# Attention units of a hybrid trunk issued from the memory's K/V projections on, with a second clock for ScalarE

## The chip, the cores and the metric

The kernel runs on one core of one Trainium2 chip (trn2). The metric is the device time of one execution in microseconds. Three executions of the kernel before gave 1529.0, 1531.52 and 1532.66; a profile of one execution stands behind all rows below.

## The reference

One decoder layer on 1024 tokens of 1024 features, all in float32. What the change touches is the first sub-layer and a part of the second:

```
a = rmsnorm(x, g_mix);  proj = a @ w_in          # q, k, v | u, v of the gating | gates
# 12 heads of 64 in 3 groups, (window, dilation) = (128,1), (512,4), (2048,16)
s = q.k * 64**-0.5 + alibi bias, masked to the window
e = exp(s - max);  den = sum(e);  o = (e @ v) / den;  lse = max + log(den)
y_attn = sum over groups of softmax(lse over groups) * o
y_sgu  = u * (w_s[group] @ rmsnorm(v, g_sgu) + b_s)      # chunks of 128 tokens
merged = gate_a * (y_attn @ w_branch_attn) + gate_s * (y_sgu @ w_branch_sgu)
h = x + merged @ w_out
# cross-attention into 256 memory tokens, 4 heads of 128
m = rmsnorm(mem, g_mem);  k, v = split(m @ w_kv_cross)
```

The rest of the layer (output of the cross-attention, SwiGLU, final norm) is not touched.

## The kernel before

Dense products are made in three terms (high by high, high by low, low by high), from operands that are split into a high part on ScalarE (an activation that copies) and a low part on VectorE (a subtraction), both on line 137 and 140 in `split`. Weights come from DRAM by SyncE's queue into one of three staging tiles (`load`, L147), are split, and are then held in one of four pairs of tiles. `next_w(ahead)` takes the next weight from a list in the order of use, and first loads and splits as many as are wanted ahead; the load and the split are written into the program at that place.

`Order` decides the order of the program while it is written. `main` is a generator that yields after each piece of TensorE work with the piece's cost, which is added to the clock `now`. Beside it stand chains (`spawn`): generators that yield (cost on TensorE, time until the next step is due). At most four chains are live, in the order in which they were spawned; after each piece of main every live chain whose time has come takes a step. `join(key)` advances the clock until the chains of that name are done.

The part of `main` that the change touches comes after the last gate projection. In a block under `tc.manual_schedule()`, inside which every engine and queue keeps the program's order, stand the loads of attention's q, k, v (`load_qk`, GpSimd's queue), of the bias table (`load_bias`), the four steps of the memory's K/V projection (`mem_kv`: steps 0 and 1 two K heads each, one weight a head; steps 2 and 3 a half of V each, two weights a step), the load of the gating's v (`sgu_load`), the spawn of `sgu_start` (transposes of the spatial weights) and, before the last K/V step, `spawn_attn`. After the block the scheduler may move instructions to where an engine is free, into the block's stretch too. There stand the norm of the gating's v, the mixing (`spatial`, four groups of channels in two halves), four branch tiles of the gating (`branch_sgu`, 48 products of 512 columns each) with a join of attention after the second, and `branch_attn`.

`spawn_attn` spawns 36 units (`attn_it`) of a pair of heads each: eight a pair in group 0, six in group 1, four in group 2. A unit has three steps: scores on TensorE (L809), bias and row minimum on VectorE (L818), exponentials with row sums on ScalarE (L820); transposes (L825) and their copy to SBUF, on ScalarE and VectorE by turns (L829, L831); products with v (L840) and, when a bank is full, its copy on ScalarE (L852). After the last unit of a group `stats(g)` transposes maxima and sums (L982), stores them (L987, SyncE) and reads them back by rows (L990, SyncE); `combine` makes the groups' weights of these, spreads them by DMA and sums the groups into y.

Of the kernel before, what the change touches and what calls it, by code (L numbers as in the profile page):

```python
# [15 lines left out]
P = 128  # L16
D = 1024
# [18 lines left out]
class Order:  # L36
    """Order of issue: a main stream of tensor-engine work, and chains of dependent steps that go between its pieces.

    A step yields (time on the tensor engine, time the other engines need before the chain's next step)."""

    def __init__(self, limit):
        self.now = 0.0
        self.limit = limit
        self.live = []
        self.waiting = []
# [4 lines left out]
    def _advance(self, th):  # L50
        try:
            cost, lat = next(th[1])
            self.now += cost
            th[0] = self.now + lat
        except StopIteration:
            self.live.remove(th)
# [29 lines left out]
def tile_hybrid_dilated_attn_sgu_gated_block(  # L86
# [90 lines left out]
    def rsqrt(ss, n, count):  # L177
        """1 / sqrt(ss / count + EPS), by columns."""
        t = [small.tile([P, 8], F32, name=f"rt{i}", tag=f"rt{i}")[:, :n] for i in range(3)]
        ms, y, q = t  # L180
        yi = small.tile([P, 8], I32, name="ryi", tag="ryi")[:, :n]
        nc.vector.tensor_scalar(ms, ss, 1.0 / count, EPS, op0=ALU.mult, op1=ALU.add)
        nc.vector.tensor_scalar(yi, ms.bitcast(I32), 1, None, op0=ALU.logical_shift_right)
        nc.vector.tensor_scalar(y.bitcast(I32), yi, -1, 0x5F3759DF, op0=ALU.mult, op1=ALU.add)
        for _ in range(3):
            nc.vector.tensor_mul(q, y, y)
            nc.vector.scalar_tensor_tensor(q, q, -0.5, ms, op0=ALU.mult, op1=ALU.mult)
            nc.vector.scalar_tensor_tensor(y, q, 1.5, y, op0=ALU.add, op1=ALU.mult)
        return y

    def neg_rsqrt(ss, n):
        """-1 / sqrt(ss / D + EPS); Newton's steps on y, each leaving it times -2, so that two operations do."""
        ms = [small.tile([P, 2], F32, name=f"nm{i}", tag=f"nm{i}") for i in range(3)]
        yi = small.tile([P, 2], I32, name="nyi", tag="nyi")
        y = small.tile([P, 2], F32, name="ny", tag="ny", bufs=4)
        q = small.tile([P, 2], F32, name="nq", tag="nq")
        for i, f in enumerate((64.0, 16.0, 4.0)):
            nc.vector.tensor_scalar(ms[i][:, :n], ss, f / D, f * EPS, op0=ALU.mult, op1=ALU.add)
            if i == 0:
                nc.vector.tensor_scalar(yi[:, :n], ms[0][:, :n].bitcast(I32), 1, None, op0=ALU.logical_shift_right)  # L200
        nc.vector.tensor_scalar(y[:, :n].bitcast(I32), yi[:, :n], -1, 0x5F3759DF, op0=ALU.mult, op1=ALU.add)
        for i in range(3):
            for c in range(n):
                nc.vector.scalar_tensor_tensor(q[:, c:c + 1], y[:, c:c + 1], ms[i][:, c:c + 1], y[:, c:c + 1],
                                               op0=ALU.mult, op1=ALU.mult)
            for c in range(n):
                nc.vector.scalar_tensor_tensor(y[:, c:c + 1], q[:, c:c + 1], -3.0, y[:, c:c + 1],
                                               op0=ALU.add, op1=ALU.mult)
        return y

    def norm_rows(srcs, hn=None, pin=False):
        """Rows times -1 / rms."""
        n = len(srcs)
        ss = small.tile([P, 8], F32, name="ss", tag="ss")
        hn = hn or [H("hn") for _ in srcs]
        for i, s in enumerate(srcs):
            a = nc.scalar.activation(hn[i], s, AF.Square, accum_out=ss[:, i:i + 1])
            if pin:
                tc.keep_in_program_order(a)
        r = neg_rsqrt(ss[:, :n], n)  # L220
        for i, s in enumerate(srcs):
            nc.vector.tensor_scalar(hn[i], s, r[:, i:i + 1], None, op0=ALU.mult)
        return hn

    def turn(hn, g, dst):
        """Two blocks of rows transposed, times -g by feature, split."""
        for kk in range(4):
# [24 lines left out]

# [1 line left out]
    plan = []  # L254
# [78 lines left out]

    # ---- Winograd's form of Strassen's product, on halves of tokens (rows), of the contraction, and of the columns, which
    # are two tiles of 128; its left operands, split ----
    QUARTERS = (("A11", "A12"), ("A21", "A22"))
# [19 lines left out]
    def sums(raw, last_big):  # L356
        """The sums of quarters, in the place of the quarters; raw(name, kk) gives these."""
        for name in ("S1", "S2", "S3", "S4"):
# [49 lines left out]
    def prod(ps, w, b, a, first):  # L408
        """(Columns of B's part b) x (rows of A's part a) into ps, or added to the sum that is there."""
        for k in range(4):  # L410
# [8 lines left out]
    def wino(out):  # L419
        """Two tiles of columns; out.c11, c22, c12, c21 take the four parts of the result, in this order: the first from  # L420
        PSUM, the others as two addends, the first of which may be overwritten."""
        w = next_w(1)
# [20 lines left out]
    def rows_weights(w_all, c0):  # L443
        """The combinations of weights for two tiles of 256 columns."""
        def part(k0, c):
# [28 lines left out]
    def prod_rows(ps, w, b, a, first):  # L474
        """As prod, rows by rows: (rows of A's part a) x (columns of B's part b)."""
        for t in range(4):
# [8 lines left out]

    def wino_rows(out):
        """As wino, for two tiles of 256 columns, features along the free axis."""
        w = next_w(0)

# [27 lines left out]

# [1 line left out]
    for q in QUARTERS[0] + QUARTERS[1]:  # L519
# [61 lines left out]
    def start():  # L581
# [21 lines left out]
        def turn_x(hn, b):  # L603
            """A block of rows transposed, split."""
            half, t = divmod(b, 4)
# [7 lines left out]
        def first(b, ps):  # L613
            """As token_major, the parts that are there first going first."""
            for n, (al, wl) in enumerate(((0, 0), (1, 0), (0, 1))):
# [4 lines left out]
        def warm(n):  # L620
            """Keeps the tensor engine busy, so that its clock is up when the data come."""
            ps = PS("warm")
# [59 lines left out]

# [1 line left out]
    qk, vts, oT = {}, {}, {}  # L684
# [47 lines left out]
    class Act:  # L732
        """An activation of each of the two tiles of columns, kept in DRAM."""

# [59 lines left out]
    def attn_it(g, pr, it, st):  # L794
# [19 lines left out]
        for (b, kbs, hh, c0, n, S_ps) in lay:  # L814
# [6 lines left out]
                                 accum_out=den[:, col:col + 1])  # L821
        yield cost, 3.0
        E_ps = PS("psE")
# [6 lines left out]
        else:  # L830
            nc.vector.tensor_copy(ET[:, :c], E_ps[:, :c])  # L831
        yield c / P * 0.107, 1.8
        for (b, kbs, hh, c0, n, _) in sorted(lay, key=lambda l: l[0]):
# [10 lines left out]
            if st[q4][1] == 8:  # L844
# [7 lines left out]
                nc.scalar.activation(o, O.rearrange("p (r i) -> p r i", r=nr), AF.Copy)  # L852
        yield c / P * 0.2, 0.0

# [17 lines left out]

# [1 line left out]
    vt_s = []  # L874
# [7 lines left out]
    class SV:  # L882
        """The gated units' v with its rows' sums of squares, kept in DRAM."""

# [81 lines left out]

    # LongNet weights of the three groups, per head and token
    sc_d = dram.tile([GROUPS, 2, HPG, S], F32, name="sc_d")
# [58 lines left out]

# [1 line left out]
    mg = [[None] * 4 for _ in range(2)]  # L1029
# [35 lines left out]

# [1 line left out]
    mem_ = {}  # L1067
# [40 lines left out]

# [1 line left out]
    h = []  # L1110
# [51 lines left out]

# [1 line left out]
    qT = {}  # L1164
# [97 lines left out]

# [1 line left out]
    raw_f, hm = {}, {}  # L1264
# [123 lines left out]
    def main():  # L1388
# [13 lines left out]
        with tc.manual_schedule():  # L1402
            load_qk(0, 0)
            load_bias()
            yield from mem_kv(0)
            sgu_load()
            yield from mem_kv(1)
            load_qk(0, 1)
            order.spawn(sgu_start(), key="sgu")
            yield from mem_kv(2)  # L1410
            spawn_attn()
            yield from mem_kv(3)
        sgu_norm()
        order.join("sgu")
        yield from spatial()
        for jj in range(2):
            yield from branch_sgu(jj)
        for g in range(GROUPS):
            order.join("attn%d" % g)
        for jj in range(2, 4):  # L1420
            yield from branch_sgu(jj)
# [74 lines left out]
```

## Time and profile before

| what | value |
|---|---|
| three executions | 1529.0, 1531.52, 1532.66 us |
| profiled execution: span, first to last instruction | 1530.7 us |
| profiled execution: time outside the span | not shown by the page |
| TensorE busy | 1490.7 us, 97% |
| VectorE busy | 980.0 us, 64% |
| ScalarE busy | 555.8 us, 36% |
| mean granted TensorE clock | 0.991 |

Busy times are shares of the whole span; they hide stages in which another engine or a transfer is the limit. The ends of matmuls are modelled, so the starts of two neighbours give the price of one. PE is TensorE, PEld its weight loads, DVE VectorE, ACT ScalarE, POOL GpSimd, SP or SPq SyncE's queue. L820 is line 820 of the kernel.

### The profile page before, as it was taken

The page shows a single profiled execution, that of the slowest core. Times are in us where ns is not written, and L with a number is a line of the kernel's source. Part 1 is how long each engine was busy: PE and PEld are TensorE (multiplying, and loading weights), DVE is VectorE, ACT ScalarE, POOL GpSimd, SP SyncE. Part 2 cuts the span into 40 slices and gives each one's busy share as a digit, 9 for nine tenths or more (in the row PEclk, how much of TensorE's full clock was granted, in tenths as well). Part 3 has the DMA queues.
Part 4 walks back from the last instruction along what each step waited for, and adds up shares of the span by engine and source line. Part 5 has one row for each costly group of instructions (what it writes and reads, how often), then busy time and mean ns, then how long its engine had stood idle before and what let it go on. Part 6 is the DMA issues. An engine that isn't in the chain of part 4 may idle for free.

```text
span 1530.7 us, 19576 instructions
## 1 busy us (share of the span) xinstructions
PE 1490.7 (97%) x7567; PEld 1247.5 (81%) x7567; DVE 980.0 (64%) x1774; ACT 555.8 (36%) x1028; POOL 138.2 (9%) x121
## 2 busy tenths in 40 slices
PE   9999999999999999899999889999999999999997
PEld 8999888888887777688888678888888888888886
DVE  7786555555456848627677975555555556776666
ACT  4335233333347742115556622222222222211124
POOL 4440000000021212200000400000000000000013
PEclk9999999999999999999999999999999999999999
DMA  6123333333495627501022122222222227332312
GB/s 218 58 92 116 110 110 110 110 110 110 138 310 193 220 55 220 186 1 55 15 66 86 56 83 83 83 83 83 83 83 83 83 97 261 110 98 85 107 52 101
DMA packets 135634, 168.54 MB, mean 110 GB/s; under 512 B 7742, under 2 KB 108850, under 8 KB 135412
## 3 DMA queue, kind: packets, MB, share of 16 engines
q1 hardware_dynamic: 122304, 125.04, 25.5%
q0 software_dynamic: 8096, 29.13, 5.7%
q10 hardware_dynamic: 5140, 13.11, 2.5%
q8 instruction: 59, 0.97, 0.3%
q14 instruction: 35, 0.29, 0.1%
HBM read 125.17 MB, written 42.09 MB: 109 GB/s over the span
## 4 chain that ended last, share of the span: by engine, by line
PE 84%; DVE 7%; DMA 4%; ACT 2%; issue 1%; POOL 1%; SPq 0%; DVEq 0%; ACTq 0%; POOLq 0%
PE psb L415 20%; PE psc L415 13%; PE psg L415 13%; PE psd L171 5%; PE psd L169 5%; PE psd L170 5%; PE pso L170 3%; PE pso L171 3%; PE pso L169 3%; DVE wl L140 2%; PE psv L170 1%; PE psv L169 1%; PE psv L171 1%; DMA wbc<-wt_d 1%; PE psb L482 1%
## 5 line engine op out<-in xcount | busy, mean ns | idle before, releaser
L137 ACT ACTIVATE wh<-wst 128x1024 fp32r<-128x1024 f32 x134 | 140.4, 1055 | 414.7 <-PE psg L415 246.9
L140 DVE TENSOR_TENSOR wl<-wst,wh 128x1024 fp32r<-128x1024 f32 x130 | 170.7, 1316 | 74.4 <-ACT wh L137 74.3
L415 PE MATMUL psg<-A,wh 128*128 128x512 f32 x592 | 183.7, 392 | 4.2 <-ACT p L426 4.2
L1367 DVE TENSOR_TENSOR h<-h,psd 128x512 f32<-128x512 f32 (+1 forms) x161 | 108.1, 682 | 60.4 <-PE psd L171 60.3
L171 PE MATMUL psd<-wh,hm 128*128 128x512 f32 (+1 forms) x356 | 137.7, 387 | 0.0
L170 PE MATMUL psd<-wl,hm 128*128 128x512 f32 (+1 forms) x356 | 137.7, 387 | 0.0
L169 PE MATMUL psd<-wh,hm 128*128 128x512 f32 (+1 forms) x356 | 137.6, 387 | 0.0
L415 PEld LDWEIGHTS psg<-A,wh 128*128 128x128 f32 x592 | 111.8, 189 | 27.7 <-ACT p L426 4.6
L415 PE MATMUL psg<-A,wl 128*128 128x512 f32 x296 | 115.7, 391 | 0.0
L415 PE MATMUL psc<-S,t 128*128 128x512 f32 x444 | 107.8, 391 | 5.9 <-DVE t L140 5.9
L415 PEld LDWEIGHTS psc<-S,t 128*128 128x128 f32 x444 | 83.8, 189 | 23.7 <-DVE t L140 6.3
L415 PE MATMUL psb<-S,t2h 128*128 128x512 f32 x296 | 92.6, 394 | 0.0
L415 PE MATMUL psc<-S,wh 128*128 128x512 f32 x296 | 91.5, 390 | 0.0
L415 PE MATMUL psb<-S,wh 128*128 128x512 f32 x296 | 91.3, 389 | 0.0
L415 PE MATMUL psb<-A,t2h 128*128 128x512 f32 x296 | 91.2, 389 | 0.0
L430 DVE TENSOR_TENSOR u<-p,psb 128x512 f32<-128x512 f32 x37 | 25.4, 687 | 97.5 <-PE psb L415 97.5
L170 PEld LDWEIGHTS psd<-wl,hm 128*128 128x128 f32 x356 | 66.9, 188 | 14.0 <-DVE wl L140 0.3
L171 PEld LDWEIGHTS psd<-wh,hm 128*128 128x128 f32 x356 | 66.9, 188 | 13.6
L169 PEld LDWEIGHTS psd<-wh,hm 128*128 128x128 f32 x356 | 66.9, 188 | 13.4
L433 DVE TENSOR_TENSOR v<-p,psc 128x512 f32<-128x512 f32 x37 | 25.4, 687 | 67.0 <-PE psc L415 67.0
L415 PEld LDWEIGHTS psb<-S,t2h 128*128 128x128 f32 x296 | 56.3, 191 | 11.9 <-ACT t2h L137 0.2
L415 PEld LDWEIGHTS psg<-A,wl 128*128 128x128 f32 x296 | 56.0, 189 | 11.7
(341 smaller groups left out, 3295.4 us busy)
## 6 DMA issues: line engine op xcount, KB each, us to landing
wst<-in_w_gate_up_dram SPq DMA_DIRECT2D x44, 512.0 KB, 4.0
wst<-in_w_in_dram SPq DMA_DIRECT2D x42, 512.0 KB, 4.7
hm_d<-hmf SPq DMA_DIRECT2D x22, 512.0 KB, 4.3
wst<-hm_d SPq DMA_DIRECT2D x22, 512.0 KB, 3.4
wst<-in_w_down_dram SPq DMA_DIRECT2D x22, 512.0 KB, 3.6
sig_d<-act ACTq DMA_DIRECT2D x16, 512.0 KB, 3.4
xin<-in_x_dram SPq DMA_DIRECT2D x8, 512.0 KB, 8.4
wst<-in_w_kv_cross_dram SPq DMA_DIRECT2D x8, 512.0 KB, 4.6
```

The source lines that it names most:

```text
L137: i = nc.scalar.activation(hi, src, AF.Copy)
L140: (eng or nc.vector).tensor_sub(lo, src, hi.bitcast(F32))
L169: nc.tensor.matmul(ps, lhsT=lh, rhs=rh, start=(i == 0), stop=False)
L170: nc.tensor.matmul(ps, lhsT=lh, rhs=rl, start=False, stop=False)
L171: nc.tensor.matmul(ps, lhsT=ll, rhs=rh, start=False, stop=(i == n - 1))
L415: nc.tensor.matmul(ps, lhsT=l, rhs=r, start=first and k == 0 and i == 0, stop=k == 3 and i == 2, skip_group_check=not first)
L430: nc.vector.tensor_add(u, p1, b)
L433: nc.vector.tensor_add(v, p1, c)
L482: nc.tensor.matmul(p, lhsT=l, rhs=r, start=first and t % 2 == 0 and k == 0 and i == 0, stop=k == 3 and i == 2, skip_group_check=not first ...
L1367: nc.vector.tensor_add(h[tb][:, ns], h[tb][:, ns], ps)
```

## The change

`Order` gets a second clock, `act`. A step of a chain may yield a third number, the time that it takes on ScalarE; the clock then goes to the later of itself and `now`, plus 1.12 times this number, and the chain's next step is due no earlier than 1.0 after it. The three steps of an attention unit yield such times, and their fixed latencies go from 3.0 and 1.8 to 2.4 and 1.5. In `main` the loads of the second pair's q and k, `sgu_start` and `spawn_attn` go ahead of the first K/V step; `sgu_load` comes after that step. The join of `sgu` goes ahead of the norm. The join of attention goes from behind the second branch tile to behind the first, so three tiles follow it. Docstrings and comments are dropped.

```diff
 class Order:
...
     def __init__(self, limit):
         self.now = 0.0
+        self.act = 0.0
...
-            cost, lat = next(th[1])
+            cost, lat, *act = next(th[1])
             self.now += cost
             th[0] = self.now + lat
+            if act:
+                self.act = max(self.act, self.now) + 1.12 * act[0]
+                th[0] = max(th[0], self.act + 1.0)
...
-        yield cost, 3.0
+        yield cost, 2.4, sum(0.28 + n / P * 0.107 for (_, _, _, _, n, _) in lay)
         E_ps = PS("psE")
...
-        yield c / P * 0.107, 1.8
+        yield c / P * 0.107, 1.5, (c / P * 0.107 + 0.15) * (st["n"] % 2)
+        evac = 0.0
...
                 nc.scalar.activation(o, O.rearrange("p (r i) -> p r i", r=nr), AF.Copy)
-        yield c / P * 0.2, 0.0
+                evac += 0.6 if d == 1 else 1.1
+        yield c / P * 0.2, 0.0, evac
...
             load_qk(0, 0)
             load_bias()
+            order.join("mem")
+            load_qk(0, 1)
+            order.spawn(sgu_start(), key="sgu")
+            spawn_attn()
             yield from mem_kv(0)
             sgu_load()
-            yield from mem_kv(1)
-            load_qk(0, 1)
-            order.spawn(sgu_start(), key="sgu")
-            yield from mem_kv(2)
-            spawn_attn()
-            yield from mem_kv(3)
+            for step in range(1, 4):
+                yield from mem_kv(step)
+        order.join("sgu")
         sgu_norm()
-        order.join("sgu")
         yield from spatial()
-        for jj in range(2):
-            yield from branch_sgu(jj)
+        yield from branch_sgu(0)
         for g in range(GROUPS):
             order.join("attn%d" % g)
+        yield from branch_sgu(1)
         for jj in range(2, 4):
             yield from branch_sgu(jj)
```

## Rows read from the trace of the kernel before

**Rows 1.** The page: span; busy time of each engine, share, instructions.
```profile
span 1530.7 us, 19576 instructions
...
PE 1490.7 (97%) x7567; PEld 1247.5 (81%) x7567; DVE 980.0 (64%) x1774; ACT 555.8 (36%) x1028; POOL 138.2 (9%) x121
```

**Rows 2.** Busy time by stage: us, each engine's busy time (count), clock, DMA.
```profile
443.40:466.70 23.30, 21.35 (x170) 20.47 (x168) 15.35 (x23) 10.97 (x15) 7.40 (x12) 1.00 0.94 321
466.70:545.80 79.10, 75.02 (x685) 56.53 (x684) 57.58 (x228) 61.24 (x207) 11.92 (x22) 1.00 0.51 180
545.80:557.40 11.60, 8.88 (x53) 5.71 (x53) 2.80 (x16) 7.30 (x28) 0.00 (x0) 0.71 0.00 1
557.40:595.00 37.60, 37.60 (x169) 31.17 (x168) 24.42 (x36) 5.80 (x6) 8.01 (x14) 1.00 0.72 195
```

**Rows 3.** TensorE's waits, 430 to 700: total us, times, longest.
```profile
PE psE L825 <- ACT T L820: 3.7, 3, 1.8
...
PE psa L169 <- ACT yAh L137: 1.6, 1, 1.6
```

**Rows 4.** Busy time in two single microseconds of the third stage.
```profile
547.00:548.00 1.00, 0.46 (x2) 0.14 (x1) 0.60 (x4) 1.00 (x4) 0.00 (x0) 1.00 0.00 0
...
550.00:551.00 1.00, 0.04 (x1) 0.00 (x0) 0.00 (x0) 1.00 (x7) 0.00 (x0) 0.50 0.00 0
```

**Rows 5.** TensorE in order of time: start, us, line, tiles, count.
```profile
443.43 0.28 PE L169 MATMUL psk<-mT,wh 128*128 128x256 f32 x1
...
446.30 0.28 PE L169 MATMUL psk<-mT,wh 128*128 128x256 f32 x1
...
522.33 0.66 PE L825 MATMUL psE<-ident,T 128*128 128x128 f32 x4
522.92 0.72 PE L809 MATMUL psS<-k,q 64*128 64x128 f32 x8
523.57 0.66 PE L840 MATMUL psO<-ET,v 128*64 128x128 f32 x8
524.16 0.66 PE L825 MATMUL psE<-ident,T 128*128 128x128 f32 x4
...
557.37 0.28 PE L982 MATMUL pst<-ident,nmx 128*32 128x128 f32 x1
...
595.03 0.39 PE L169 MATMUL psa<-yAh,wh 128*128 128x512 f32 x1
```

**Rows 6.** ScalarE in order of time, one split of a weight.
```profile
476.23 1.06 ACT L137 ACTIVATE wh<-wst 128x1024 fp32r<-128x1024 f32 x1 [3.62 <-DMA wst<-in_w_branch_sgu_dram]
```

**Rows 7.** VectorE in order of time, the second low half of y.
```profile
598.00 1.22 DVE L140 TENSOR_TENSOR yAl<-oT,yAh 128x1024 fp32r<-128x1024 f32 x1
```

**Rows 8.** GpSimd's queue, the bias table's second transfer, and both transfers' landing.
```profile
434.19 0.55 POOL L578 DMA_DIRECT2D bias<-in_bias_tab_dram  x1
...
DMA to landing us min/median/max: 7.6/7.6/7.7
```

**Rows 9.** SyncE's queue around the statistics of groups 1 and 2.
```profile
534.74 0.77 SPq L987 DMA_DIRECT2D sc_d<-stT  x2
539.62 3.60 SPq L990 DMA_DIRECT2D stat<-sc_d  x8
558.31 0.78 SPq L987 DMA_DIRECT2D sc_d<-stT  x2
559.74 3.63 SPq L990 DMA_DIRECT2D stat<-sc_d  x8
```

**Rows 10.** The page's DMA issues: count, KB each, us to landing.
```profile
wst<-in_w_kv_cross_dram SPq DMA_DIRECT2D x8, 512.0 KB, 4.6
```

**Rows 11.** VectorE in order of time, the mixing's three operations.
```profile
494.69 0.74 DVE L958 SCALAR_TENSOR_TENSOR m<-psm,colc,sguc 128x512 f32<-128x512 f32 x1
...
496.48 0.68 DVE L962 TENSOR_TENSOR m<-m,u 128x512 f32<-128x512 f32 x1
...
498.03 0.68 DVE L140 TENSOR_TENSOR yS<-m,yS 128x512 fp32r<-128x512 f32 x1
```

## Prediction

> **What bounds the kernel now.** I read the page first: TensorE is busy for 97% of the span [rows 1], so a change of order can only win where TensorE waits or runs slowly. The chain of waits showed where the two spans of dense products end and the mixed stretch between them begins, about 440 to 630 us. I cut this stretch into stages with the table by windows [rows 2]. The reader is to see four different stages in it: the memory's projections (443.4 to 466.7), attention with the gating's mixing and the first branch tile in between (466.7 to 545.8), the last attention units alone (545.8 to 557.4), and branch tiles alone (557.4 to 595.0). ScalarE fills 61.2 of 79.1 us in the second and TensorE's clock averages 0.71 in the third; in the fourth TensorE is busy throughout. TensorE's own list of waits [rows 3] then names what it waited for, and finer windows [rows 4] show the clock at 0.50, the lower of its two levels, after a while in which ScalarE was full and TensorE half idle. The timeline of TensorE [rows 5] gave prices from one start to the next, since its ends overlap.
>
> Prices. 24 K/V products take 446.30 - 443.43 = 2.87, so one costs 0.12 us and a piece of three 0.36. A full attention unit costs 0.65 for its scores, 0.59 for its transposes and 0.59 for its products with v, in sum 1.83 [rows 5]. A branch product costs (595.03 - 557.37 - 0.15) / 165 = 0.227 us [rows 5].
>
> **The change, part by part.** No matmul, activation or transfer is added or dropped; docstrings and comments make no instruction. What changes is the order, which I worked through with the queue's own rule: a step that is due goes between two pieces of the main stream, four chains at a time, and after the change not before ScalarE's modelled clock allows it.
>
> *Removed, first stage.* 55 pieces at 0.36 and four transposes at 0.15 are 20.4 us of work in 23.3 us [rows 2, 5]: 2.9 us are lost where V's weights are split on ScalarE and VectorE no faster than they are used (TensorE stands idle for 1.95 of them, the rest is in the gaps from start to start). With attention units between the pieces, each weight has several times as long. I take 2.9; bounds 0 and 2.9.
>
> *Removed, second stage.* The longest wait for T is 1.8 us [rows 3]: ScalarE stood 3.62 us at the split of a branch weight whose transfer was late, with the exponentials queued behind it [rows 6]. Now the first branch weight comes behind the attention. I take 1.8; bounds 0 and 1.8. The small waits left over in this stage, about 2 us, I leave in both kernels.
>
> *Removed, third stage.* The work between 545.8 and 557.4 is 12 transposes of four-block tiles and 32 products: 1.77 + 1.18 + 0.59 + 0.59 + 0.59 for attention and 0.68 for three branch products, 5.4 us. It takes 11.6 [rows 2], so 6.2 are lost, to ScalarE's chain of exponentials and to the low clock [rows 4]. After the change the last units stand between the mixing's products and the first branch tile, so this tail is gone. I take 6.2; bounds 3 and 6.2.
>
> *Removed, before the attention branch.* The weights of the groups start with two transposes at 557.37 and end with the split of the second y at 598.00 + 1.22 = 599.2, 41.9 us later [rows 5, 7]. TensorE has 37.5 us of branch tiles for this and then loses 1.6 to the wait for yAh [rows 3] and some 0.9 more around it, 2.5. After the change three tiles and all but two pieces of a fourth follow these transposes: 62 x 0.68 = 42.3 us. That just covers 41.9. I take 2.5; bounds 0 and 2.5.
>
> Sum removed: 2.9 + 1.8 + 6.2 + 2.5 = 13.4 us.
>
> *Inputs that are asked for sooner.* The first unit now comes some 2 us after 443.4. The bias table is issued at 434.19 and lands 7.6 later, at 441.8 [rows 8]; q, k and v are ahead of it in the same queue. Nothing here; if the cover fails, each microsecond of lateness is one on TensorE.
>
> *Added: loads behind the group statistics.* This is the term I trust least. In the old order all four steps of K/V issue their weight loads before any statistics. In the new order group 0 finishes after the second K step, so its statistics go into SyncE's queue ahead of the loads of V's second and third weight, and the block in which this happens keeps program order on every queue. In program order a statistic is a store, four reads of it, a second store, four reads. From the transposes to the first store pass 0.94 us, its data are there 1.43 later, eight reads take 3.63, so four take 1.8 [rows 9]. Step by step: 0.94 + 1.43 + 1.8 = 4.2, then 1.43 + 1.8 more: the queue is free 7.4 us after the transposes. A K/V weight lands 4.6 after issue [rows 10], at 12.0; ScalarE needs 1.06 to split it [rows 6]: 13.1. TensorE is there sooner: after the transposes the plan has two products with v, one set of transposes, three sets of scores (3.7 us), then four K/V pieces and three attention steps (3.2), 7.1 with the statistics' own. So it waits 6.0, then about 0.9 for the low half and 1.1 for an ET copy that is queued on VectorE behind both splits: 8.0 us. ScalarE's and VectorE's queues stand at the same split, so the units behind can't fill it; mixing products (0.9 each, eight of them) can, since work outside the block may be put into its gaps. Bounds: 0, if these fill it, and 17: 8.0, with both stores landing as late as in group 1 (539.62 - 534.74 = 4.9 in place of 1.43 [rows 9]), which adds 6.9, and 2 for a low clock. Between them I take 5: half of the hole filled, some clock lost.
>
> The row's 1.43 us for a small store is what I count with. The Trainium skill, DMA: Bandwidth & Descriptors, section Latency and other measured facts, gives about 2 us as the fixed cost of a transfer; by that the two landings would add 1.1 us and the wait would be an estimated 9.1 in place of 8.0.
>
> *Added: the mixing at the end.* Before, its eight halves were spread through attention. Now they come after it, in 7.2 us of products plus some 3.5 of attention steps. VectorE needs 0.74 + 0.68 + 0.68 per half by duration [rows 11], about 0.08 less for each where its neighbour follows at once, so 1.86, and 14.9 in all, and the first branch tile wants the fourth channel group 2 us after it starts. 14.9 - 10.7 - 2 = 2.2; I take 2, bounds 0 (mixing put forward into holes) and 5 (ET copies and weight splits in the same queue).
>
> *Added: splits between exponentials.* Seven weight splits of 1.06 on ScalarE [rows 6] are not in its modelled clock. With four chains live most hide; I take 1, bounds 0 and 4.
>
> Net: 13.4 - 5 - 2 - 1 = 5.4 us off. The profiled span is 1530.7; the page gives no time around it, and the median of the three runs, 1531.5, is 0.8 above. So 1531.5 - 5.4 = 1526.1.
>
> **The rivals.** *Late loads covered* (chance 0.2): the mixing products or early loads fill the hole and nothing else is new; 13.4 - 3 = 10.4 off, 1521.1. For it: work from outside the block can go ahead; against it: ScalarE and VectorE are stuck too, so their copies of those products wait.
>
> *Given back* (0.19): the hole stays open at 8.0 and the clock falls for it, 10 in sum; with 2 and 1 that is 13 of 13.4, 1531.1, no change that can be told. For it: the queue order above. Against it: it needs every filler to fail.
>
> *Slower* (0.15): one mechanism, SyncE's queue behind group 0's statistics. If both stores land in 4.9 us, V's second weight is 6.9 us later, the hole is 15 plus 2 for the clock, and 17 + 3 - 13.4 gives 6.6 us more, 1538.1. It decides from a hole of 10.4 us on, and past 13.5 the change is measurably slower. For it: group 1's store did take 4.9. Against it: group 2's took 1.43, and at that place few transfers are queued. The clock speaks for it too: with little to do from about 547 on it stood at 0.50 from 550 on [rows 4]. The Trainium skill, TensorE: Matmul & The Clock Gate, section HAM oscillation, says that a pause of this sort returns the array to half rate, so that a wait costs more than its length; the trace agrees, at 0.50.
>
> **How the numbers follow.** The forecast, one hole half filled, has 0.46, and its own range is 3.5 to 9 us off, 1522.5 to 1528. A measurement of this kernel can tell some 0.2%, 3.1 us. Faster: 0.46 + 0.2 = 0.66, same 0.19, slower 0.15. The range from 1518 (all 13.4 won) to 1534 leaves out the worse half of the slower case and a little else.
>
> **What would show it.** Right: no stretch at 0.5 clock with ScalarE full between the last scores and the first branch tile; no wait for yAh; TensorE waiting for wl or wh of the memory's V behind group 0's statistics, with SyncE issuing that load after eight small reads; VectorE dense in the mixing. The prediction is wrong if V's second weight is issued before the statistics, if that wait is over 11 us, or if attention waits on ScalarE all along the K/V pieces, which would say that the new spacing is too tight.

## The result, and the profile after

The change made the kernel slower: 1541.65 us (median of four executions, 1540.91 to 1545.05) against 1531.93 for the kernel before. The ratio is 1.0072, interval 1.006 to 1.0084; the forecast was 1526.1, a gain. The profiled execution took 1545.05 us, 1.65 over its span, which is 12.7 us longer than the span of before [rows 1]. It is the slowest of the four, 3.4 us above their median, so the pieces read from it below add up to somewhat more than the 9.7 us between the medians. The page:

```profile
span 1543.4 us, 19576 instructions
...
PE 1490.1 (97%) x7567; PEld 1251.5 (81%) x7567; DVE 976.8 (63%) x1774; ACT 555.3 (36%) x1028; POOL 136.8 (9%) x121
```

The work is the same to the instruction, so the difference is waiting and clock. To see where it lies I cut both traces at the first TensorE product of four kinds, read from TensorE's timeline: K/V of the memory (psk), attention branch (psa), output projection (pso), query projection (psq).

| | first psk at | psk to psa | psa to pso | pso to psq | psq to the end |
|---|---|---|---|---|---|
| before | 443.43 | 151.6 | 24.6 | 96.3 | 814.8 |
| after | 445.20 | 155.8 | 34.3 | 93.9 | 814.3 |

The 1.8 us ahead of psk stand in front of the changed code (psk begins between 442.6 and 447.3 in the other profiles of this case), 4.2 are lost up to the attention branch, 9.7 within it, and 2.4 come back behind it. TensorE's waits from 430 to 700 us, with total, times and longest; of those of before, [rows 3] shows two, and its wait for ml follows. (yAh and yAl are the high and low half of attention's y, wh and wl of a weight, wo of an output weight, mh and ml of the merged branches; ET are the transposed exponentials.)

```profile
PE psa L174 <- ACT yAh L142: 10.8, 1, 10.8
PE psv L174 <- ACT wh L142: 7.3, 1, 7.3
PE psO L846 <- DVE ET L836: 3.9, 4, 2.0
PE pso L176 <- DVE ml L145: 2.6, 2, 1.8
```

Before:

```profile
PE pso L171 <- DVE ml L140: 4.0, 3, 2.4
```

Two single waits make the difference: one of 7.3 us for the high half of a V weight, and one for the second y that grew from 1.6 to 10.8. Both in TensorE's timeline (a number in brackets is the idle time ahead of the row and what ended it):

```profile
496.99 0.60 PE L830 MATMUL psE<-ident,T 128*128 128x128 f32 x4
504.85 0.58 PE L174 MATMUL psv<-wh,mT 128*128 128x256 f32 x1 [7.26 <-ACT wh L142]
506.11 0.58 PE L175 MATMUL psv<-wl,mT 128*128 128x256 f32 x1 [0.68 <-DVE wl L145]
...
508.19 1.12 PE L846 MATMUL psO<-ET,v 128*64 128x128 f32 x8 [0.64 <-DVE ET L836]
...
601.00 0.39 PE L174 MATMUL psa<-yAh,wh 128*128 128x512 f32 x1
...
613.12 0.80 PE L174 MATMUL psa<-yAh,wh 128*128 128x512 f32 x1 [10.82 <-ACT yAh L142]
```

SyncE's queue shows why the first weight was late, and the last three rows why the second y was:

```profile
491.76 0.34 SPq L994 DMA_DIRECT2D sc_d<-stT  x1
494.84 1.71 SPq L997 DMA_DIRECT2D stat<-sc_d  x4
496.59 0.42 SPq L994 DMA_DIRECT2D sc_d<-stT  x1
498.10 1.69 SPq L997 DMA_DIRECT2D stat<-sc_d  x4
499.83 1.52 SPq L152 DMA_DIRECT2D wst<-in_w_kv_cross_dram  x3
...
578.55 1.75 SPq L1026 DMA_DIRECT2D wbc<-wt_d  x3
593.65 0.36 SPq L152 DMA_DIRECT2D wst<-in_w_out_dram  x1
594.18 1.78 SPq L1026 DMA_DIRECT2D wbc<-wt_d  x3
```

The three K/V loads leave only when store, four reads, store, four reads of group 0 are out, 9.3 us after the first of their transposes at 490.53. Later, SyncE's second batch of broadcast weights (wbc) stands behind the load of an output weight, which waits 13 us for a staging tile. VectorE holds that tile and closes the circle:

```profile
592.41 1.22 DVE L145 TENSOR_TENSOR wl<-wst,wh 128x1024 fp32r<-128x1024 f32 x1
...
604.72 1.23 DVE L1027 TENSOR_TENSOR oT<-oT,wbc 128x1024 f32<-128x1024 f32 x1 [8.17 <-DMA sig<-sig_d]
...
613.63 1.22 DVE L145 TENSOR_TENSOR yAl<-oT,yAh 128x1024 fp32r<-128x1024 f32 x1
```

The low half of the second attention-branch weight frees the tile at 593.6. ScalarE had its high half at 580.3, but VectorE's order puts the low half behind the multiplications with the first batch of wbc. So the second batch leaves at 594.18, and the low half of the second y ends at 614.85, 56.3 us after the transposes of group 2. Before it was 41.9 [rows 5, 7], with the second batch at 578.00:

```profile
578.00 1.73 SPq L1019 DMA_DIRECT2D wbc<-wt_d  x3
```

(The releaser printed at 604.72 is the last by the profile; the operand is wbc.)

Windows around both holes, with TensorE's busy time first and its granted clock behind the five engines, against [rows 2, 4]:

```profile
500.00:505.00 5.00, 0.15 (x1) 0.15 (x1) 0.17 (x1) 1.06 (x1) 3.35 (x7) 0.50 0.82 256
505.00:510.00 5.00, 3.68 (x18) 2.72 (x18) 2.88 (x3) 2.50 (x3) 0.00 (x0) 0.50 1.05 364
510.00:515.00 5.00, 5.00 (x37) 3.81 (x35) 2.35 (x13) 2.92 (x10) 0.00 (x0) 0.63 1.02 400
530.00:550.00 20.00, 19.96 (x205) 17.50 (x203) 15.37 (x69) 19.10 (x72) 2.94 (x7) 1.00 0.60 185
605.00:610.00 5.00, 0.00 (x0) 0.00 (x0) 4.80 (x5) 0.00 (x0) 0.00 (x0) 0.59 0.01 5
610.00:615.00 5.00, 1.88 (x5) 1.52 (x6) 5.00 (x7) 2.00 (x2) 0.00 (x0) 0.50 0.16 33
```

Each hole is followed by work at the lower level. Behind the first, TensorE works 3.68 us at 0.50 and 5.00 us at 0.63 on average, and 3.68 x 0.50 + 5.00 x 0.37 = 3.7 us are lost by it. The tail at low clock of before is gone: TensorE is full at 1.00 from 530 to 550, and from there to the first branch tile at 557.1 it is busy for 5.40 of 7.10 us, still at 1.00.

### The profile page after: what moved, and what is told of

Its sections match the earlier page's. It is cut to its first block, busy times and chain, and to the rows that moved or that the text cites. A ratio compares the mean times of both kernels' runs of the same rounds, so it can differ in the third digit from the quotient of the medians.

```text
span 1543.4 us, 19576 instructions
## 1 busy us (share of the span) xinstructions
PE 1490.1 (97%) x7567; PEld 1251.5 (81%) x7567; DVE 976.8 (63%) x1774; ACT 555.3 (36%) x1028; POOL 136.8 (9%) x121
## 4 chain that ended last, share of the span: by engine, by line
PE 87%; DVE 4%; ACT 3%; DMA 2%; issue 1%; POOL 1%; SPq 0%; DVEq 0%; ACTq 0%; POOLq 0%
PE psb L420 20%; PE psc L420 13%; PE psg L420 13%; PE psd L175 5%; PE psd L176 5%; PE psd L174 5%; PE pso L176 3%; PE pso L174 3%; PE pso L175 3%; PE psv L175 1%; PE psv L174 1%; PE psv L176 1%; PE psb L487 1%; ACT T L825 1%; PE psq L176 1%
```

## The experiments

All times stand against the kernel before on the same chip, with the 95% interval of the ratio; the changed kernel's ratio is 1.0072, and differences to it are taken from the ratios. The segments are those of the table above.

**The two queues, one at a time.** First the statistics on GpSimd's queue, alone:

```diff
-            nc.sync.dma_start(sc_d[g, w_]...
+            nc.gpsimd.dma_start(sc_d[g, w_]...
-                nc.sync.dma_start(      # stat
+                nc.gpsimd.dma_start(
```

> The statistics of the groups (two stores and eight reads each) are issued on GpSimd's queue in place of SyncE's. Theory: the loads of V's last weights stood behind group 0's statistics in SyncE's queue; with the statistics elsewhere they are issued before TensorE reaches them, the wait of 7.3 us for the weight's high half at the split goes, with 0.7 for its low half, 0.6 for ET and 1 to 3 us of low clock behind them: 9.5 us less than the changed kernel, about 1532. The wait for yAh of 10.8 us stays, since the statistics of group 2 are not in its chain. Rival, that ScalarE and VectorE set the pace of the attention units whatever comes when: the waits spread over exponentials and ET copies, the sum of waits in 445 to 560 us falls by less than 3 us, time 1538.5 or more. Rival, that the hole only moves: GpSimd's queue now holds the mixing's adds behind its own DMA issues, TensorE waits for these, 1538 or more.

Measured 1533.93 us, ratio 1.0002 (0.9987 to 1.0017): 0.7% less than the changed kernel, 10.7 us. Its waits:

```profile
PE pso L176 <- DVE ml L145: 7.1, 1, 7.1
...
PE psa L174 <- ACT yAh L142: 1.4, 1, 1.4
...
PE psv L174 <- ACT wh L142: 0.8, 1, 0.8
```

The first hole went as the theory had it. Beyond it, the wait for yAh went too, which I had not expected: VectorE's instructions came into another order, the low half of the second attention-branch weight at 571.23, ahead of the multiplications, and wbc's second batch left at 575.01. In return the wait for ml rose from 2.6 to 7.1. So this run removes both holdups, and gives 4.5 us back. That the time came out near the expected 1532 is luck, as the expectation counted the first hole alone.

The same queue with its waits shortened: both stores ahead of the eight reads, all on SyncE.

```diff
+        for w_ in range(2):
             nc.sync.dma_start(sc_d[g, w_]...
+        for w_ in range(2):
             src = ...   # four reads
```

> All of the statistics stay on SyncE's queue, but both stores are issued ahead of the eight reads, so that the queue waits once for a landing and not twice. Theory of the queue held by group 0's statistics: the loads of V's last weights are issued some 1.4 to 1.7 us sooner (the second wait of 1.69 us overlaps the first), so the hole of 7.3 us shrinks by about as much and the time by 1.5 to 3 us: 1539.5. If the hole has nothing to do with the queue, it stays at 7.3 us and the time at 1541.6.

Measured 1541.0 us, 1.0052 (1.0034 to 1.0069). The hole follows the queue, as the theory asks; it shrinks by 2.3 us, a little more than expected. The time is lower by 3 us, but the two intervals overlap:

```profile
PE psv L174 <- ACT wh L142: 5.0, 1, 5.0
```

The other holdup alone: wbc on GpSimd's queue.

```diff
-                    (nc.sync, nc.gpsimd)[hh].dma_start(t[hh * HD:(hh + 1) * HD, :], ...
+                    nc.gpsimd.dma_start(t[hh * HD:(hh + 1) * HD, :], ...
```

> The broadcast loads of the groups' weights (wbc) are all issued on GpSimd's queue; before, half of them went to SyncE's. Theory: the second batch stood on SyncE behind the load of an output weight, which waited until VectorE had split the second attention-branch weight, and that split stood behind multiplications with the first batch. Without that circle the second batch is issued at about 580 in place of 594, the second y is split before 601, and the wait for yAh (10.8 us) goes with the clock drop around it: 10 us less than the changed kernel, about 1531.5. The hole of 7.3 us at 497 to 505 stays. Rival, that the wait for yAh is the length of the combining chain itself (transposes, statistics, landing, multiplications; VectorE's work on branch weights among it): it falls by less than 4 us, time 1538 or more.

Measured 1538.4 us, 1.0035 (1.0024 to 1.0046), 5.7 us less than the changed kernel where 10 were expected:

```profile
PE psv L174 <- ACT wh L142: 6.7, 1, 6.7
PE pso L176 <- DVE ml L145: 6.5, 1, 6.5
...
PE psa L174 <- ACT yAh L142: 1.4, 1, 1.4
```

The wait for yAh falls by 9.4 us as the theory says, the first hole stays, and 3.9 us come back at ml. Both moves together:

> Both moves together: the statistics and all the broadcast loads on GpSimd's queue. Theory: the two holdups lie in different stretches (497 to 508 and 602 to 613 us) and add: 9.5 and 10 us, 19.5 us less than the changed kernel, 1522, and so some 10 us faster than the kernel before. Rival, that they cover for each other (what is won in the first is waited for again at the second, since the chain to yAh starts with the same transposes): 1528 to 1533. Rival, that all of it on one queue makes that queue the bound: 1535 or more.

Measured 1535.24 us, 1.0015 (1.0002 to 1.0029). The 1522 of the theory is far off. By the number it is the rival of a queue as the bound (1535 or more). By the waits it is rather the rival that gains cover for each other, since with the same queue and another order of the splits (the last run below) the wait for yAh falls to 1.2:

```profile
PE psa L174 <- ACT yAh L142: 6.3, 1, 6.3
...
PE pso L176 <- DVE ml L145: 2.0, 3, 0.9
```

From psk to psa it needs 145.1 us, 10.7 less than the changed kernel and 6.5 less than before. In all three kernels with a moved queue, the waits for yAh and ml add up to about 8 us (8.5, 7.9, 8.3; before 5.6).

**Other places, other spacing.** Attention started after both K steps, and after the first:

```diff
-            spawn_attn()
             yield from mem_kv(0)
             sgu_load()
-            for step in range(1, 4): yield from mem_kv(step)
+            yield from mem_kv(1)
+            spawn_attn()
+            yield from mem_kv(2)
+            yield from mem_kv(3)
```

> The changed kernel, but attention starts after the two K steps of the memory's projections (24 of 55 pieces later), and all else as changed. The loads of all V weights then stand ahead of group 0's statistics in SyncE's queue. Theory of the held queue: the hole of 7.3 us before V's products and the wait for yAh (10.8 us) both go, the tail at low clock stays gone, and VectorE's full stretch before the output projection keeps a wait for ml of about 6.5 us: 9 to 14 us less than the changed kernel, 1530 (1527 to 1533). Rival, that the loss comes from attention's spacing or from mixing being left for the end: these are the same here, so 1538 or more.

> As changed, but attention starts after the first K step. Three of V's four weights are then loaded ahead of group 0's statistics, and only the last stands behind them. Theory of the held queue: TensorE reaches the last weight a V step later than the queue lets it go, so the hole before V's products is below 2 us; time 1531 to 1534. If the hole depends on the amount of attention that ScalarE has to do by then and not on the queue, it is between that of the changed kernel (7.3 us) and that of the start after both K steps: 1535 to 1539.

After both: 1542.34 us, 1.0061 (1.0043 to 1.0079), and not the 1530 of the theory. The late hole before V is gone as it had it, but six waits for high and low halves of K/V weights between 452 and 469 us take 8.1 us, yAh 3.5 and ml 6.9. By the number this is the rival; whether spacing or the late mixing has a part in it, the run doesn't show, and why those K/V weights come late is open. After the first: 1558.47 us, 1.0168 (1.0145 to 1.0192), worse than either end. Only V's last weight stands behind the statistics there, and TensorE waits 7.7 us for it: one late weight makes the whole hole, against my expectation of 2. Another wait of 7.5 us, for maxima (nmx) near 465 us, has the same form: ScalarE stands 7.9 us for the landing of a K weight before it splits it at 461.98, VectorE stands 8.5 us for the low half, and the maxima queue behind.

The two halves of the change apart: the new places with the old spacing (steps due after 3.0 and 1.8 us, nothing for ScalarE), and the old places with the new clock.

> As changed in the order of the main stream, but without the second clock: attention's steps are spaced as before (3.0 and 1.8 us, no account of ScalarE's time). With four chains from the start and nothing that holds them back, attention takes most of the slots between the first K pieces, ScalarE falls behind, and V's weights stand behind the statistics of all groups. Theory: slower than the changed kernel by 5 us or more, 1547 to 1560, so the second clock is not what costs. Rival, that the spacing by the second clock is the loss: faster than the changed kernel, 1538 or less.

> The second half of the change alone: attention, K/V and branch tiles in the places of the kernel before, with the second clock for ScalarE in the spacing. No K/V load stands behind statistics here, and the mixing lies among attention's steps. If the early places are what costs, this is near before, 1529 to 1535; the stall of the last K/V steps (2.9 us) is back, and attention's tail is longer or shorter by how the spacing falls. Rival, that the spacing itself costs (fewer units under the mixing, a longer tail at low clock): 1538 or more.

The new places with the old spacing took 1579.92 us, 1.031 (1.0285 to 1.0335), beyond the 1547 to 1560 expected, with one wait of 27.1 us for a V weight: K/V products give way to attention, and V's last weight loads behind the statistics of all three groups. The old places with the new clock took 1539.75 us, 1.0058 (1.0038 to 1.0078); the spacing stretches attention there, the transposes of group 2 come 128.0 us behind psk in place of 113.9 [rows 5], and TensorE waits twice for yAh, 7.4 us in all. I had expected it near before. So the early start without the second clock costs far more than with it, the second clock in the old places is no gain either, and each half alone is slower than before, as both together are.

**What the repaired kernels wait for.** In the kernel with the statistics on GpSimd, ml made ahead of two low halves of output weights:

```diff
-        wo = [next_w(0) for _ in range(6)]
+        wo = [next_w(0) for _ in range(4)]
         ...
         prep(0)
-        wo += [next_w(0) for _ in range(2)]
+        wo += [next_w(0) for _ in range(4)]
```

> The kernel with the statistics on GpSimd's queue, and in it the first block's split of the merged branches (mh, ml) is traced ahead of the fifth and sixth output weight: VectorE then makes ml ahead of two low halves of weights (4.5 us together in that kernel's profile); nothing else changes its place. Theory that VectorE's full stretch before the output projection is what took back part of the gain: the wait for ml falls from 7.1 us to 2.5 to 3.5, the low clock behind it (0.83 over 620 to 640 us) mostly goes, and the time falls by 4 to 5 us to about 1529, some 0.2% below the kernel before. Rival, that the wait for ml only turns into one for the low halves of those weights right behind it: the sum of waits at the output projection stays at 6 to 7 us and the time within 1 us of 1534.

> The kernel before with the same two repairs: statistics on GpSimd's queue, and ml ahead of two low halves of output weights. Before had no K/V load behind the statistics and a wait for ml of 4.0 us in all. If the repairs only mend what the change broke, before gains 0 to 2 us: 1530 to 1532, and the changed kernel with repairs (expected 1529) keeps a gain of 1 to 3 us from the early start. Rival, that the repairs are good for before just as much: 1527 to 1529, and the early start of attention is worth nothing by itself.

Measured 1535.32 us, 1.0016 (1.0002 to 1.0029): the rival. The wait changes its name to that of a weight whose load waited for a staging tile:

```profile
PE pso L174 <- ACT wh L142: 4.2, 1, 4.2
...
PE psa L174 <- ACT yAh L142: 3.3, 1, 3.3
...
PE pso L176 <- DVE ml L145: 1.9, 2, 1.0
```

Before with the same two repairs took 1535.4 us, 1.0022 (1.0008 to 1.0036): there they cost 3 us, 2.0 of them behind the first query projection (816.8 in place of 814.8; the last section has the reason). They are no general gain.

Four low halves of output weights moved from VectorE to GpSimd:

```diff
-                              tuple(t[:, k % 2, :] for t in wo_big))
+                              tuple(t[:, k % 2, :] for t in wo_big), eng=nc.gpsimd)
```

> The kernel with the statistics on GpSimd's queue, and in it the low halves of the first four output weights are made on GpSimd in place of VectorE (four subtractions of 1.22 us on VectorE). In that kernel the waits at the two holes had fallen to 0.8 and 1.4 us, but one of 7.1 us for ml had come up at the output projection, with VectorE full from 588 to 629 us. Theory that VectorE's work of that stretch is now the bound: 4.9 us less of it, the wait for ml falls to 2 to 4 us and the time by 3 to 5 us, to about 1530. Rival, that the wait for ml is set by the loads of the output weights, which wait for staging tiles: GpSimd frees these later, the wait stays at 7 us or grows, 1534 or more.

Measured 1539.52 us, 1.0052 (1.0031 to 1.0073): neither. The wait for ml fell to 3.4 us, but yAh waited 8.7. While GpSimd worked on its three subtractions (588.82 to 597.8), VectorE's rows read:

```profile
589.32 2.99 DVE L1027 TENSOR_TENSOR oT<-oT,wbc 128x1024 f32<-128x1024 f32 x1
592.23 0.68 DVE L1053 TENSOR_TENSOR mg<-mg,psb 128x512 f32<-128x512 f32 x1
592.83 2.78 DVE L1027 TENSOR_TENSOR oT<-oT,wbc 128x1024 f32<-128x1024 f32 x1
595.53 3.36 DVE L1028 TENSOR_TENSOR oT<-oT 128x1024 f32<-128x1024 f32 x1
```

The three on tiles of 1024 columns take 1.22 us elsewhere in this trace, so VectorE lost 5.5 us on them, more than the 4.9 that four low halves take there. What GpSimd took over, VectorE lost.

**VectorE relieved without GpSimd.** The low halves of all eight output weights as plain copies on ScalarE, in the kernel with both moves and in the kernel before. The copies leave out the subtraction, so these kernels do not do the whole computation:

```diff
-        (eng or nc.vector).tensor_sub(lo, src, hi.bitcast(F32))
+        nc.scalar.activation(lo, src, AF.Copy) if eng is nc.scalar else ...   # eng=nc.scalar for w_out
```

> The kernel with both repairs on GpSimd's queue, and in it the low halves of the eight output weights are made by ScalarE, as plain copies of the weight, in place of VectorE's subtraction (this part of the computation is changed, for its time only). VectorE has 8 x 1.22 = 9.8 us less to do between the second y and the output projection, ScalarE, idle for two thirds of that stretch, 8 x 1.06 = 8.5 us more. Theory that VectorE bounds this stretch: the waits for yAh (6.3 us) and ml (2.0 us) fall to 3 us or less together, and the time from 1535.2 to about 1529. Rival, that late loads (three staging tiles for all weights) set the pace: the waits change their names but keep a sum of 6 us or more, and the time stays at 1533 or more.

> The same edit to the kernel before (low halves of the eight output weights as plain copies on ScalarE, nothing else). If VectorE bounds the same stretch there, the waits for ml (4.0 us) and yAh (1.6 us) fall to 2 us or less together and the time falls by 3 to 4 us, to about 1528: then both kernels stand before the same limit, and of what the change wins in front of it only that is kept which starts VectorE's work sooner. If before is not under this limit, it stays within 1 us of 1531.9.

Before gained somewhat more than expected: 1526.22 us, 0.9965 (0.9952 to 0.9977), with the wait for ml gone and that for yAh as it was (1.8). VectorE's work on these weights does bound this stretch there. The changed kernel did not: 1534.5 us, 1.0017 (1.0006 to 1.0027). ml fell to 1.9, but yAh waited 7.3. VectorE's timeline shows that it was ready:

```profile
594.38 1.22 DVE L1029 TENSOR_TENSOR oT<-oT 128x1024 f32<-128x1024 f32 x1
602.81 1.23 DVE L145 TENSOR_TENSOR yAl<-oT,yAh 128x1024 fp32r<-128x1024 f32 x1 [7.20 <-ACT yAh L142]
```

ScalarE made yAh at 601.74, behind output weights that it had to wait for. The last two runs put each split of an output weight behind the second y in its engine's order, with VectorE relieved and with its full work:

```diff
-        split(st[:, :n], ...)
+        with tc.issue_after(yAh), tc.issue_after(yAl): split(st[:, :n], ...)   # w_out only
```

> The kernel with both repairs and the low halves of the eight output weights as plain copies on ScalarE (that part of the computation is changed, for its time only), and in it every split of an output weight stands behind the second y in the order of its engine; only ScalarE's order differs. Theory that the second y stood behind late output weights on ScalarE: the wait for yAh falls from 7.3 us to 2 or less, the low clock behind it (0.84 over 600 to 620 us) goes too, and the time falls from 1534.5 to about 1527, level with the kernel before under the same relief of VectorE (1526.2). If the early start is worth something of its own once everything behind it is relieved, it comes out below that: 1524 or less. Rival, that the y is late for another reason: the wait stays above 5 us and the time above 1532.

> The kernel with both repairs, nothing left out, and every split of an output weight behind the second y in the order of its engine. The wait for yAh falls from 6.3 us to 2 or less, as three low halves of 1.2 us come behind the second y on VectorE. Theory that VectorE's amount of work is the limit of this stretch: the same 6 us come back as waits for ml or for low halves of weights at the output projection, and the time stays at 1533 to 1536. Rival, that only the order was bad: the sum of waits at yAh and ml falls from 8.3 to 4 us or less, and the time to about 1530, faster than before by 0.1%.

Relieved: 1531.37 us, 0.9994 (0.998 to 1.0008); yAh fell to 1.2 as expected, yet the time is not the expected 1527 but 0.3% above that of before under the same relief. VectorE now stands where a gate is late, which GpSimd loads behind one of its additions, and ml comes behind it:

```profile
612.37 0.69 DVE L1070 TENSOR_TENSOR sig<-sig,psa 128x512 f32<-128x512 f32 x1 [4.41 <-DMA sig<-sig_d]
```

With full work: 1535.88 us, 1.0028 (1.0019 to 1.0037), and all that was won at yAh is waited for at ml:

```profile
PE pso L176 <- DVE ml L145: 8.3, 1, 8.3
...
PE psa L174 <- ACT yAh L142: 1.2, 1, 1.2
```

No kernel that does the whole computation beat the one before.

## Why the prediction was wrong

*The step that failed: the wait for yAh.* In "Removed, before the attention branch" I set TensorE's 42.3 us of branch tiles against the 41.9 us of the old combining chain and took 2.5 us as won. The first number was right: TensorE came to the attention branch 42.4 us after the transposes. The second was read from the trace of before as if it were a property of the chain. It was one of an order: wbc behind an output weight's load, that behind a low half on VectorE. After the change this order gave 56.3 us. In place of 2.5 us won, the wait grew by 9.2 us, the largest term of the outcome; the spreads on another queue took it away.

*The term that was mis-sized: loads behind the statistics.* The mechanism and the place were right. 8.0 us were worked out; 7.3 + 0.7 + 0.6 = 8.6 us were measured, and the clock behind it cost 3.7, where I had 2 in the bound only. That 8.0 came so near is in part luck: the wait for the high half was 7.3 and not 6.0, as the data of the first store took 3.1 us from its issue (491.76 to 494.84) and not 1.43, and the two terms behind it were 1.3 and not 2.0. I then entered 5, for mixing products that would fill half of the hole. None did: the first came at 544.66, after all of V. The rival "given back" had the hole open; that ScalarE and VectorE stand at the same split stood in the term itself, and I counted on fillers against it. Why the mixing came so late no run shows. The statistics elsewhere and the shortened queue show the mechanism of the hole by removal and by dose.

*What was right.* The tail at low clock is gone, and with the first hole removed, psk to psa takes 145.1 to 149.3 us against 151.6, 2.3 to 6.5 less. My terms for this part come to 2.9 + 1.8 + 6.2 - 2 - 1 = 7.9, a little more than the best of these. With the hole they fit the changed kernel too: 8.6 + 3.7 - 7.9 = 4.4 us lost, 4.2 measured. VectorE is dense in the mixing, as said.

*What I left out.* Time won ahead of the attention branch counts only if VectorE's work behind it also moves. In the repaired kernels VectorE is busy for 34.6 to 37.5 of the 40 us from 590 to 630, and before for all of 600 to 620:

```profile
600.00:620.00 20.00, 20.00 (x90) 16.37 (x88) 20.00 (x21) 5.99 (x9) 8.09 (x5) 1.00 0.53 177
```

An early TensorE just waits there, 7.9 to 12.1 us at yAh and the output projection in the six kernels that have a moved queue and the full work. That VectorE bounds before in this stretch is shown by the run that relieved it (5 us less). In the changed kernel three things were shown one behind the other: queue, order on ScalarE, VectorE's work (0.3% between the last two runs). How much of that work is its amount and how much is time that GpSimd's additions take from it, no run separates; the traces have an estimate in the last section.

The relieved changed kernel stays 0.3% behind the relieved kernel before, and the two profiles show where. From psk to psa it is 4.7 us ahead. From psa to psq it takes 120.3 us against 115.0, by the two last waits for ml (2.9 and 0.4) and some 1.4 of low clock behind them (0.92 and 0.91 over 610 to 630). Behind psq it loses 2.4 more (817.0 against 814.5), which is the price of the moves to GpSimd's queue and not of the early start: before with the statistics moved has 816.8 there. So 2.1 to 2.6 us of the repaired kernels' times belong to the repair itself, and the two relieved kernels are not quite compared like with like.

*Slower by which rival.* The forecast's "slower" asked for a first hole of 13.5 us. It had 8.6 + 3.7 = 12.3, by the forecast's sum 1.9 us slower, which can't be told from no change. The second holdup, which no rival named, and the gains lost at VectorE make up the rest.

## What to carry to other kernels

A step that is moved past others in an in-order queue brings its waits with it: list what stands behind each DMA that waits for a landing or for a free tile, on the queue after the move, and don't count on other engines to fill the gap if they stand at the same operand. A chain's length in the old trace includes the order in which it was served; before setting "it just covers" against it, follow its links (queue, staging tile, the engine that frees the tile) under the new order. And look one stage further: what TensorE wins ahead of a stretch where another engine is full is waited for there. Before work or transfers go to GpSimd, look at which VectorE operations run beside it and at the end of the program: here the work cost VectorE more than it was to save, and the transfers cost 2.1 to 2.6 us at the end.

## What the runs showed of the hardware

GpSimd and VectorE hold each other up: a VectorE operation on two SBUF operands took 2.78 to 3.36 us in place of 1.22 while GpSimd subtracted, and the three subtractions took 3.0 us each. The Trainium skill, SBUF — State Buffer, section Who interferes with whom, says that a VectorE instruction with two SBUF inputs contends with a GpSimd instruction that reads SBUF; the trace agrees, and the multiplications with a PSUM operand kept their pace (0.68 us at 592.23, in the middle of the subtractions, as elsewhere).

The same holds without any experiment, in the kernel before, where GpSimd makes four additions of the merged branches:

```profile
605.70 2.41 POOL L1064 TENSOR_TENSOR mg<-mg,sig 128x1024 f32<-128x1024 f32 x1 [19.25 <-DVE sig L1063]
```

```profile
606.78 2.40 DVE L140 TENSOR_TENSOR wo<-wst,wo 128x1024 fp32r<-128x1024 f32 x1
```

Beside them three low halves of weights take 2.40, 3.04 and 3.03 us in place of 1.22, and three of ml 3.27 in place of some 1.1. By these rows the four additions cost VectorE an estimated 7.0 us of the stretch that bounds the kernel; made on VectorE at 1.22 each they would take 4.9. In the last run, with its wait of 8.3 us for ml, the same count gives 4.1 us. No run moves the additions, so what that would win is not shown.

A DMA on GpSimd's queue has a price at the end of the program. GpSimd's last long instruction is a DRAIN, which lasts 7.22 us in the kernel before and 9.67 with the 30 DMAs of the statistics on its queue:

```profile
L1492 POOLq DRAIN  x3: 46/93/7224, 1522.3 to 1530.4; - x3
```

```profile
L1499 POOLq DRAIN  x3: 46/98/9673, 1522.0 to 1532.2; - x3
```

With the six of wbc it lasts 7.72, with both 10.17, and it is the same to 0.01 us in all kernels with the same number, so some 0.08 us for each DMA. With 30 or 36 more it ends last: from TensorE's last product to the end pass 9.4 us before, 11.5 with the statistics moved and 12.0 with both, and that is all that these kernels lose behind psq.

The granted clock differs between kernels with nearly the same waits. The kernel with the statistics on GpSimd, in one window (TensorE's busy time first, the clock behind the five engines):

```profile
470.00:480.00 10.00, 10.00 (x79) 7.50 (x81) 4.40 (x18) 6.71 (x25) 0.00 (x0) 0.83 0.15 50
```

The kernel with both moves, on the same chip and with the same order of TensorE's work up to there:

```profile
470.00:480.00 10.00, 7.96 (x70) 5.60 (x69) 7.23 (x24) 5.80 (x19) 0.00 (x0) 1.00 0.17 55
```

TensorE waits 2.0 us for the same ET at 469 and at 473 us; the clock falls behind the one and not behind the other, and again between 490 and 510 (0.90 and 0.76 against 1.00). From psk to psa they take 149.3 and 145.1 us. Such a price can't be read from one execution: the twelve of the first kernel took 1529.04 to 1537.01 us.
